# One ring place, three load orders and the folds of a two-layer block kernel

## The chip, the cores and the metric

The kernel runs on one core of a Trainium2 chip. A core has a matrix engine (TensorE, PE in the profile, with its weight loads as PEld) and four more engines with queues of their own: VectorE (DVE), ScalarE (ACT), GpSimd (POOL) and SyncE (SP, which here issues all transfers). The metric is the time of one execution on the device in microseconds.

## The reference

Two layers over 512 latent tokens and 256 context tokens, width 1024, feed-forward width 4096, float32. Cut to what matters here:

```python
for i in range(2):
    sh1, sc1, g1, sh2, sc2, g2 = split(silu(c) @ w_ada[i] + b_ada[i])   # and the same for ctx from c_ctx
    a = window_gqa(...) if i == 0 else diff_attention(...)
    x = layer_norm(alpha * x + g1 * a, ln1_g[i], ln1_b[i])
    fx = square(relu((x * (1 + sc2) + sh2) @ w1[i])) @ w2[i]
    x = layer_norm(alpha * x + g2 * fx, ln2_g[i], ln2_b[i])
    # layer 0 does the same to ctx; layer 1 needs only x
```

## The kernel before

**Numbers.** Each float32 product is made of three matmuls on values split in a rounded high part and the rest (mm3, L325 high x high, L326 and L327 the mixed ones). So every weight has to be prepared: a transfer brings it into a raw buffer, ACT rounds it (w_h, L264), DVE subtracts (w_l, L314); only then may PE use it. `wsplit` does that. Raw buffers come from a ring of three (tag raw, NRAW = 3); w_h and w_l from rings of four each (NH = 4).

**The order of work.** A planner in Python (class `Flow`) walks through jobs, with a cost for every operation and a latency after it (LNLAT = 6.0 us after a layer norm's normalise), and writes PE's order by hand from that. The order on ACT, DVE, POOL and SP is set by a scheduler by priority, which goes mostly by the place in the program. Each engine takes its queue strictly in order: what stands behind a waiting instruction waits too. All loads go through SP's one queue.

**The MLP (`mlp_pipe`).** It works on token blocks (tb) of 128: six in layer 0, four in layer 1. Blocks 0 to 5 of w1 are done plainly (`plain`). After that come the *pairs* q = 3 to 15 (`pair`): two blocks of w1 (a1, a2, the pair's raws) are quartered and combined to seven half weights (A11, A12, S2, S1, S3, S4, A22) so that seven products replace eight. POOL makes the sums (w_sum and sums in place, `part_sums`); `half` casts a half on ACT and subtracts on DVE into a tile w_half, and takes a place in the ring rhalf that PE gives back when the product (12 matmuls) is done. Between the products stand y groups: products of the second matrix w2 (y_ps), two weights for each of 7 chunks c and two halves of the 1024 columns. `sink` adds them to a tile fx; `fold` multiplies fx by the gate and adds it to the residual acc, both on POOL. `last_y` does the last chunk, whose sums `final` adds (`gated_add`: g_tmp on DVE at L583, then the add on DVE or POOL), and after half 1 of a block comes its layer norm (`moments`, `normalise` at L534, `ln_job`, which ends in transposes xn_t on PE, L549).

**Where things lie.** In layer 0 the pairs' two w1 raws are tiles of their own, and a half weight's tile is taken in turn from four pools (raw, bc, wh, wl): every fourth half lies in one of the three raw buffers. These also hold the y weights and the rows of w_adaT, the modulation of later stages, which the `filler` loads and DVE sums (custom instructions at L260), one step each time `R0.extra` draws. In layer 1 a fourth raw buffer, in the pool of its MLP, takes part in the rotation of all raws.

**The ends.** Layer 0's MLP ends with six loads of acc from m_spill (`tail`), two gate loads (g), the folds, the last y groups, and six layer norms, while `pre1` starts the qkv products of layer 1's attention. Layer 1's MLP begins with the last attention output weight (b_wo), the acc loads and the layer norm rows.

Of the kernel before, what the change touches and what calls it, by code (L numbers as in the profile page):

```python
# [19 lines left out]
P = 128  # L20
# [214 lines left out]
def hybrid_block(ctx: ExitStack, tc: tile.TileContext, t: dict, out: bass.AP):  # L235
# [296 lines left out]
    def normalise(a, st, dep):  # L532
        mv, rstd, d = moments(st, dep)
        nc.vector.tensor_scalar(out=a, in0=a, scalar1=mv[:, 0:1], scalar2=rstd, op0=ALU.subtract, op1=ALU.mult)  # L534
        return fl.op("D", dve(620), [d], LNLAT)


    def ln_job(pool, acc, tb, hx, A, B, ready, st, dep, keep=None):
        dep = normalise(acc, st, dep)
# [156 lines left out]
    def mlp_pipe(l, hx, ready, ntok, acc, get_gates, done, fx, T, R):  # L696
# [220 lines left out]
        def sink(c, half, tb, pt, p, slot):  # L917
            x = fx[tb][:, half * 512:half * 512 + 512]
            if (half, tb) not in fresh:
                fresh.add((half, tb))  # L920
                sm_.give(slot, ac(512, [p], nc.scalar.copy, out=x, in_=pt))
                if half == 0 and R.res:
                    R.res.pop(0)()
                return
            d = dv(512, [p], nc.vector.tensor_tensor, out=x, in0=pt, in1=x, op=ALU.add)
            sm_.give(slot, d)
            if c == 6 - half and gates:
                fold(half, tb, d)
# [13 lines left out]
        def last_y():  # L942
            def final(half, tb, pt, p, slot):
                r = gated_add(R.pool, lambda x: sm_.give(slot, x), acc[tb], half, pt, p, gates[0 if tb < NXB else 1],
                              half == 1 or l == 0)
# [17 lines left out]
            yield from before(1)  # L963
            if not gates:
                gates.extend((yield from get_gates()))
                for half in range(2):
                    for tb in range(ntb):
                        fold(half, tb, None)
# [61 lines left out]
        y_weights(0, 0)  # L1030
        y_weights(0, 1)
        weights(3, 4)
# [414 lines left out]
    with tc.tile_pool(name="mlp0", bufs=1, reuse_waits="tile") as pool:  # L1447
# [26 lines left out]
        class R0:  # L1474
            rhalf = Ring(fl, 4)
# [10 lines left out]
            def half_tile(self, n):  # L1486
                p_, tag, b = ((wpool, "raw", NRAW), (pool, "bc", 2), (wpool, "wh", NH), (wpool, "wl", NH))[n % 4]
                return p_.tile([P, 1024], F32R, name="w_half", tag=tag, bufs=b)
# [24 lines left out]
            def extra(self):  # L1513
                self.turn += 1
                if self.turn % 5 in (1, 3):
                    next(filler, None)
# [18 lines left out]
        def done2(tb, st, r):  # L1535
# [6 lines left out]
            fl.add(ln_job(pool, acc[tb], tb, st2["hx"], st2["A"], st2["B"], ready2, st, r), 0)  # L1542
# [379 lines left out]
    with tc.tile_pool(name="mlp1", bufs=1, reuse_waits="tile") as pool:  # L1922
        xraw["pool"] = pool
# [36 lines left out]
        class R1:  # L1960
# [4 lines left out]
            def pair_raws(self):  # L1965
                return raw_tile(), raw_tile()
# [107 lines left out]
```

## Time and profile before

| | |
|---|---|
| time, median of 3 runs | 1671.41 us (1671.11 to 1679.01) |
| the profiled execution's own time | 1669.35 us |
| its span, first to last instruction | 1667.6 us |
| granted TensorE clock, mean | 0.983 |
| PE busy | 1572.0 us, 94% |
| DVE, ACT, POOL busy | 1141.7, 790.1, 448.2 us |
| layer 0's MLP, pairs | about 455 to 815 us |
| layer 0's end, qkv of layer 1 | about 815 to 915 us |
| layer 1's MLP, pairs | about 1320 to 1620 us |

The profile is of one execution. In a row of a timeline stand the start, the duration, engine, line, operation, what it writes and reads, and in brackets how long the engine stood before it and what ended that. In a row of the waits stand the engine and line, what it waited for, the sum in us, how often, and the longest. A merged row (x2 and more) lasts from the first start to the last end.

### The profile page before, as it was taken

How to read it: one execution, taken by the hardware profiler on the slowest of the kernel's cores; microseconds unless marked ns; L12 is line 12 of the kernel's file. 1: busy time of each engine (PE TensorE's matmuls, PEld its weight loads, DVE VectorE, ACT ScalarE, POOL GpSimd, SP SyncE). 2: the span in 40 equal slices, each digit the busy share in tenths (PEclk: the TensorE clock that was granted, in tenths of full speed). 3: DMA queues.
4: the chain of work that ended last, by engine and by line, in shares of the span. 5: the costliest groups of instructions: out<-in, count | busy, mean ns of one | idle time of the engine just before them, and what ended most of it. 6: DMA issues, size and time to landing. Idle time of an engine off the chain costs nothing. (4 is left out here: it accounts for less than half of the span.)

```text
span 1667.6 us, 25133 instructions
## 1 busy us (share of the span) xinstructions
PE 1572.0 (94%) x9465; PEld 1385.1 (83%) x9465; DVE 1141.7 (68%) x2204; ACT 790.1 (47%) x1683; POOL 448.2 (27%) x364
## 2 busy tenths in 40 slices
PE   7899999999989997999998998999989899999997
PEld 5787777789878986988978898999877779999886
DVE  4555677699777687766486777776755875556577
ACT  3465676364433342334417555555542735555450
POOL 1334454106112111211550222221000033333463
PEclk9999999999999998999999999999999999999999
DMA  9110551533454334532522122211114332233221
GB/s 372 40 51 33 181 174 39 184 146 108 138 165 152 126 131 140 160 127 89 181 76 97 47 68 70 65 45 39 48 51 152 103 113 90 101 103 101 97 92 51
DMA packets 66434, 181.17 MB, mean 109 GB/s; under 512 B 7368, under 2 KB 13320, under 8 KB 66312
## 3 DMA queue, kind: packets, MB, share of 16 engines
q1 hardware_dynamic: 66312, 179.56, 31.6%
q8 instruction: 74, 1.21, 0.3%
q14 instruction: 48, 0.39, 0.1%
HBM read 168.49 MB, written 11.04 MB: 108 GB/s over the span
## 5 line engine op out<-in xcount | busy, mean ns | idle before, releaser
L325 PE MATMUL y_ps<-w_h,hid 128*128 128x512 f32 (+1 forms) x648 | 254.2, 392 | 15.2 <-ACT w_h L264 14.2
L326 PE MATMUL y_ps<-w_l,hid 128*128 128x512 f32 (+1 forms) x648 | 254.8, 393 | 6.7 <-DVE w_l L314 6.7
L327 PE MATMUL y_ps<-w_h,hid 128*128 128x512 f32 (+1 forms) x648 | 252.9, 390 | 0.0
L314 DVE TENSOR_TENSOR w_l<-w_raw,w_h 128x1024 fp32r<-128x1024 f32 (+1 forms) x133 | 164.0, 1242 | 81.8 <-ACT w_h L264 80.0
L264 ACT CAST w_h<-w_raw 128x1024 fp32r<-128x1024 f32 (+1 forms) x133 | 131.8, 1000 | 160.9 <-PE y_ps L327 64.0
L268 POOL TENSOR_TENSOR w_sum<-w_raw 128x512 f32<-128x512 f32 x26 | 57.6, 2217 | 478.6 <-DMA w_raw<-in_w 330.1
L325 PEld LDWEIGHTS y_ps<-w_h,hid 128*128 128x128 f32 x648 | 123.2, 190 | 39.5 <-ACT w_h L264 15.5
L326 PEld LDWEIGHTS y_ps<-w_l,hid 128*128 128x128 f32 x648 | 123.1, 190 | 31.4 <-DVE w_l L314 9.9
L264 ACT CAST w_half<-w_raw 128x512 fp32r<-128x512 f32 x130 | 78.5, 619 | 140.0 <-PE h_ps L327 69.8
L327 PEld LDWEIGHTS y_ps<-w_h,hid 128*128 128x128 f32 x648 | 123.1, 190 | 25.7
L325 PE MATMUL qkv_ps<-w_h,hx 128*128 128x384 f32 (+1 forms) x384 | 128.4, 334 | 0.6 <-ACT qT L264 0.5
L260 DVE TENSOR_TENSOR w_half<-w_raw,w_half 128x512 fp32r<-128x512 f32 x130 | 101.6, 795 | 39.0 <-ACT w_half L264 38.5
L327 PE MATMUL qkv_ps<-w_h,hx 128*128 128x384 f32 (+1 forms) x384 | 123.3, 321 | 0.0
L326 PE MATMUL qkv_ps<-w_l,hx 128*128 128x384 f32 (+1 forms) x384 | 123.2, 321 | 0.0
L268 POOL TENSOR_TENSOR e<-e,sm 128x512 f32<-128x512 f32 (+2 forms) x96 | 92.7, 979 | 108.4 <-DVE sm L260 89.8
L260 DVE TENSOR_TENSOR fx<-y_ps,fx 128x512 f32<-128x512 f32 x110 | 75.4, 686 | 49.8 <-PE y_ps L327 49.7
L260 DVE CUSTOM_DVE_ANT_0 w_raw<-w_raw,cB 128x512 f32<-128x512 f32 x112 | 81.5, 758 | 26.8 <-DMA w_raw<-in_w_adaT 26.7
L264 ACT ACTIVATE relu<-relu 128x384 f32<-128x384 f32 (+3 forms) x104 | 69.5, 671 | 50.6 <-DVE relu L260 49.3
L268 POOL TENSOR_TENSOR rope<-rope,rope 128x256 f32<-128x256 f32 (+1 forms) x40 | 35.3, 883 | 213.2 <-DVE rope L260 169.7
L264 ACT ACTIVATE e<-e,nm 128x513 f32<-128x513 f32 (+2 forms) x96 | 65.9, 687 | 32.9 <-DVE nm L260 26.2
L325 PE MATMUL h_ps<-hx1m,w_half 128*128 128x256 f32 x260 | 74.2, 286 | 7.1 <-DVE relu L260 4.0
L325 PEld LDWEIGHTS qkv_ps<-w_h,hx 128*128 128x128 f32 x384 | 73.3, 191 | 2.2 <-issue 1.2
(267 smaller groups left out, 4287.6 us busy)
## 6 DMA issues: line engine op xcount, KB each, us to landing
w_raw<-in_w SPq DMA_DIRECT2D x128, 512.0 KB, 3.6
w_raw<-in_w_adaT SPq DMA_DIRECT2D x56, 512.0 KB, 3.9
w_raw<-in_w_ada SPq DMA_DIRECT2D x24, 512.0 KB, 3.8
w_raw<-in_b_w SPq DMA_DIRECT2D x32, 384.0 KB, 3.3
raw<-in_w_ada SPq DMA_DIRECT2D x16, 512.0 KB, 9.6
w_raw<-in_a_wq SPq DMA_DIRECT2D x8, 512.0 KB, 7.0
w_raw<-in_a_wo SPq DMA_DIRECT2D x8, 512.0 KB, 4.3
w_raw<-in_b_wo SPq DMA_DIRECT2D x8, 512.0 KB, 4.7
```

The costliest lines, as they stand in the source:

```text
L260: fn(**kw)
L264: fn(**kw)
L268: fn(**kw)
L314: last["split"] = nc.vector.tensor_tensor(**kw)
L325: nc.tensor.matmul(out=o, lhsT=lh, rhs=rh, start=start, stop=False, **kw)
L326: nc.tensor.matmul(out=o, lhsT=lh, rhs=rl, start=False, stop=False, **kw)
L327: last["pe"] = nc.tensor.matmul(out=o, lhsT=ll, rhs=rh, start=False, stop=stop, **kw)
```

## The change

It does the following.

- Layer 0: the ring rhalf has three places (was four), and a half weight's tile is taken from bc, wh and wl in turn; no half lies in a raw buffer.
- `R0.extra` draws a step of the filler in three of eight turns (was two of five).
- Layer 1: the raws of all weights rotate over three buffers; the second raw of a pair has one buffer of its own in the pool of the MLP.
- In layer 1 the loads of pair 3's w1 are written ahead of the second y weights.
- `sink` folds only half 0, at chunk 6. Half 1 is folded in `last_y`, written behind the sums of the pairs.
- `final` in layer 0: half 0 and the last block add on DVE, half 1 of the other five blocks on POOL (all on DVE before). In layer 1 as before.
- The planner counts a latency of 2.5 us instead of 6.0 for the last block's layer norm at the end of layer 0.

The diff:

```diff
--- before.py
+++ after.py
@@ -529,14 +529,14 @@
         d = gp(0.47, [d], nc.gpsimd.tensor_tensor, out=rstd, in0=rstd, in1=mhalf[:, 0:1], op=ALU.pow)
         return mv, rstd, d
 
-    def normalise(a, st, dep):
+    def normalise(a, st, dep, lat=LNLAT):
         mv, rstd, d = moments(st, dep)
         nc.vector.tensor_scalar(out=a, in0=a, scalar1=mv[:, 0:1], scalar2=rstd, op0=ALU.subtract, op1=ALU.mult)
-        return fl.op("D", dve(620), [d], LNLAT)
-
-
-    def ln_job(pool, acc, tb, hx, A, B, ready, st, dep, keep=None):
-        dep = normalise(acc, st, dep)
+        return fl.op("D", dve(620), [d], lat)
+
+
+    def ln_job(pool, acc, tb, hx, A, B, ready, st, dep, keep=None, lat=LNLAT):
+        dep = normalise(acc, st, dep, lat)
         s = 0 if tb < NXB else 1
         tok = slice(tb * P, (tb + 1) * P)
         rs = []
@@ -924,7 +924,7 @@
                 return
             d = dv(512, [p], nc.vector.tensor_tensor, out=x, in0=pt, in1=x, op=ALU.add)
             sm_.give(slot, d)
-            if c == 6 - half and gates:
+            if c == 6 and gates:
                 fold(half, tb, d)
 
         def y_groups(groups):
@@ -942,7 +942,7 @@
         def last_y():
             def final(half, tb, pt, p, slot):
                 r = gated_add(R.pool, lambda x: sm_.give(slot, x), acc[tb], half, pt, p, gates[0 if tb < NXB else 1],
-                              half == 1 or l == 0)
+                              half == 1 if l else half == 0 or tb == ntb - 1)
                 st[tb], r = stats(acc[tb], half, r, st.get(tb))
                 if half:
                     done(tb, st[tb], r)
@@ -961,11 +961,12 @@
             y_weights(7, 0)
             yield from before(0)
             yield from before(1)
+            halves = (1,) if gates else (0, 1)
             if not gates:
                 gates.extend((yield from get_gates()))
-                for half in range(2):
-                    for tb in range(ntb):
-                        fold(half, tb, None)
+            for half in halves:
+                for tb in range(ntb):
+                    fold(half, tb, None)
             for tb in range(ntb):
                 yield sm_.ok
                 pt, slot = psm("y_ps"), sm_.take()
@@ -1028,8 +1029,10 @@
             for _ in sums:
                 pass
         y_weights(0, 0)
+        if l == 0:
+            y_weights(0, 1)
+        weights(3, 4)
         y_weights(0, 1)
-        weights(3, 4)
         yield from steps(2 * ntb)
         for q in range(3, 16):
             if q == R.gate_at:
@@ -1472,7 +1475,7 @@
             fl.add(ln_job(pool, acc[tb], tb, hx, A, B, ready, st, r, fx[tb]), 0)
 
         class R0:
-            rhalf = Ring(fl, 4)
+            rhalf = Ring(fl, 3)
             mixes = ((2, 2, 2, 0), (4, 4, 4, 0))
             gate_at, res = 16, None
             ahead, done, turn = 1, 0, 0
@@ -1484,7 +1487,7 @@
                 return self.ws
 
             def half_tile(self, n):
-                p_, tag, b = ((wpool, "raw", NRAW), (pool, "bc", 2), (wpool, "wh", NH), (wpool, "wl", NH))[n % 4]
+                p_, tag, b = ((pool, "bc", 2), (wpool, "wh", NH), (wpool, "wl", NH))[n % 3]
                 return p_.tile([P, 1024], F32R, name="w_half", tag=tag, bufs=b)
 
             def relu_tile(self):
@@ -1512,7 +1515,7 @@
 
             def extra(self):
                 self.turn += 1
-                if self.turn % 5 in (1, 3):
+                if self.turn * 3 % 8 < 3:
                     next(filler, None)
 
         def main0():
@@ -1539,7 +1542,8 @@
                 st2["hx"] = hx_big("hx1")
             if tb == NTB - 1:
                 st2["last"] = True
-            fl.add(ln_job(pool, acc[tb], tb, st2["hx"], st2["A"], st2["B"], ready2, st, r), 0)
+            fl.add(ln_job(pool, acc[tb], tb, st2["hx"], st2["A"], st2["B"], ready2, st, r, None,
+                          LNLAT if tb < NTB - 1 else 2.5), 0)
 
 
         def pre1():
@@ -1920,7 +1924,6 @@
         fl.run()
 
     with tc.tile_pool(name="mlp1", bufs=1, reuse_waits="tile") as pool:
-        xraw["pool"] = pool
         hl = [late.tile([P, 1024], F32R, name="w_" + x, tag="w" + x, bufs=1) for x in "hl"]
         acc = [pool.tile([P, D], F32, name="acc1", tag="acc", bufs=NXB) for _ in range(NXB)]
         for tb in range(NXB):
@@ -1963,7 +1966,7 @@
             gate_at, ahead = 10, 2
 
             def pair_raws(self):
-                return raw_tile(), raw_tile()
+                return raw_tile(), (pool.tile([P, 1024], F32, name="w_raw", tag="raw", bufs=1), rraw1.get(), rraw1)
 
             def sum_tile(self):
                 return late.tile([P, 1024], F32, name="w_sum", tag="wh", bufs=1)
```

What moves is told by the order of instructions. **SP, in the pairs of layer 0**, a stretch of nine loads with what each waits for. in_w1 are a pair's raws, in_w2 a y weight, in_w_adaT rows of the filler; DMAHW is an earlier transfer's end. Before:

```order
L275 DMA w_raw_4058<-in_w1 128x1024 [waits DVE_49]
L275 DMA w_raw_4059<-in_w1 128x1024 [waits DMAHW3_49]
L275 DMA w_raw_5409<-in_w_adaT 128x2x512 [waits DMAHW4_49,DMAHW1_49,DVE_49]
L275 DMA w_raw_5434<-in_w_adaT 128x2x512 [waits PE_49]
L275 DMA w_raw_5468<-in_w2 128x1024 [waits DMAHW5_49,DVE_49]
L275 DMA w_raw_5481<-in_w_adaT 128x2x512 [waits DMAHW7_49,DMAHW6_49,DVE_49]
L275 DMA w_raw_5506<-in_w_adaT 128x2x512 [waits PE_49]
L275 DMA w_raw_5544<-in_w2 128x1024 [waits DMAHW7_49,DVE_49]
L275 DMA w_raw_5605<-in_w_adaT 128x2x512 [waits DMAHW2_49,DMAHW0_49,DVE_49]
```

and now:

```order
L275 DMA w_raw_5460<-in_w2 128x1024 [waits DMAHW2_49,DMAHW1_49,DVE_49]
L275 DMA w_raw_5473<-in_w_adaT 128x2x512 [waits DMAHW3_49,DVE_49]
L275 DMA w_raw_5498<-in_w_adaT 128x2x512 [waits DMAHW4_49,DVE_49]
L275 DMA w_raw_5536<-in_w2 128x1024 [waits DMAHW5_49,DMAHW3_49,DVE_49]
L275 DMA w_raw_4058<-in_w1 128x1024 [waits DMAHW7_49,DVE_49]
L275 DMA w_raw_4059<-in_w1 128x1024 [waits DVE_49]
L275 DMA w_raw_5604<-in_w_adaT 128x2x512 [waits DMAHW4_49,DVE_49]
L275 DMA w_raw_5648<-in_w_adaT 128x2x512 [waits DMAHW0_49,DVE_49]
L275 DMA w_raw_5673<-in_w_adaT 128x2x512 [waits DMAHW2_49,DMAHW1_49,DVE_49]
```

Before, some loads wait for PE, to which a raw buffer with a half weight belongs; now loads wait for DVE and for earlier transfers.

**PE, at the end of layer 0**, around the transposes xn_t of the last blocks (acc_7904, 7905 and 7906 are blocks 3, 4 and 5). Now it reads:

```order
L325 MATMUL y_ps<-w_h,hid 128x512
L326 MATMUL y_ps<-w_l,hid 128x512
L327 MATMUL y_ps<-w_h,hid 128x512
L549 MATMUL xn_t<-identr,acc_7904 128x128 x4
L549 MATMUL xn_t<-identr,acc_7905 128x128 x8
L325 MATMUL qkv_ps<-w_h,hx_8181 128x384
L326 MATMUL qkv_ps<-w_l,hx_8181 128x384
L327 MATMUL qkv_ps<-w_h,hx_8181 128x384
L325 MATMUL qkv_ps<-w_h,hx_8181 128x384
L326 MATMUL qkv_ps<-w_l,hx_8181 128x384
L327 MATMUL qkv_ps<-w_h,hx_8181 128x384
L549 MATMUL xn_t<-identr,acc_7906 128x128 x8
L325 MATMUL qkv_ps<-w_h,hx_8181 128x384
```

The first rows are the last y matmuls. Before, 18 qkv matmuls stood between those and the transposes of acc_7905, and 54 more ahead of those of acc_7906:

```order
L325 MATMUL qkv_ps<-w_h,hx_8181 128x384
L326 MATMUL qkv_ps<-w_l,hx_8181 128x384
L327 MATMUL qkv_ps<-w_h,hx_8181 128x384
L549 MATMUL xn_t<-identr,acc_7906 128x128 x8
```

So the last block's transposes moved ahead of 66 of the 72 qkv matmuls.

**SP, in layer 1's MLP**, at pair 4 (w_raw_13620 and 13621 are its w1, 13639 and 13645 y weights, l2g and l2b the layer norm's rows). Before:

```order
L275 DMA w_raw_13620<-in_w1 128x1024
L275 DMA w_raw_13621<-in_w1 128x1024
L275 DMA l2g_16231<-in_lnrow 128x1024
L275 DMA l2b_16233<-in_lnrow 128x1024
L275 DMA w_raw_13639<-in_w2 128x1024
L275 DMA w_raw_13645<-in_w2 128x1024
L275 DMA w_raw_13823<-in_w1 128x1024
L275 DMA w_raw_13848<-in_w2 128x1024
```

and now:

```order
L275 DMA w_raw_13620<-in_w1 128x1024
L275 DMA w_raw_13639<-in_w2 128x1024
L275 DMA w_raw_13645<-in_w2 128x1024
L275 DMA l2g_16231<-in_lnrow 128x1024
L275 DMA l2b_16233<-in_lnrow 128x1024
L275 DMA w_raw_13823<-in_w1 128x1024
L275 DMA w_raw_13842<-in_w2 128x1024
L275 DMA w_raw_13621<-in_w1 128x1024
```

The two y weights moved ahead of l2g and l2b, the pair's second w1 behind them. At the start of that MLP, some 20 loads earlier, the first three loads of w1 stood ahead of the four of acc and of the last attention output weight (b_wo); now they stand behind these.

## The prediction

> **What bounds the kernel now.** I read first the page's busy times, then the waits of TensorE (PE), then the span in windows of 30 us, and then the timeline at the longest stalls.
>
> ```profile
> span 1667.6 us, 25133 instructions
> PE 1572.0 (94%) x9465; PEld 1385.1 (83%) x9465; DVE 1141.7 (68%) x2204; ACT 790.1 (47%) x1683; POOL 448.2 (27%) x364
> PE y_ps L325 <- ACT w_h L264: 16.1, 4, 9.5
> PE y_ps L326 <- DVE w_l L314: 7.5, 8, 2.5
> PE h_ps L325 <- DVE relu L260: 4.0, 1, 4.0
> ```
>
> PE is busy 94% and bounds the kernel, so a change can win only the 95.6 us in which it stands (1667.6 - 1572.0), and the time that it runs at a lower clock. The largest waits are those of the second MLP matrix (y_ps) for its cast (ACT, w_h) and its low part (DVE, w_l). The windows tell where. Columns: PE, PEld, DVE, ACT, POOL busy with counts, granted clock, DMA share, GB/s.
>
> ```profile
> 480.00:510.00 30.00, 25.52 (x120) 22.33 (x119) 20.83 (x39) 11.13 (x18) 6.52 (x4) 0.94 0.47 156
> 510.00:540.00 30.00, 28.15 (x139) 24.87 (x139) 19.76 (x37) 11.07 (x17) 4.28 (x3) 1.00 0.52 177
> 540.00:570.00 30.00, 30.00 (x153) 27.31 (x152) 22.79 (x42) 11.86 (x19) 7.20 (x5) 1.00 0.45 141
> 630.00:660.00 30.00, 22.76 (x113) 20.06 (x112) 23.37 (x58) 8.98 (x14) 4.38 (x4) 0.97 0.32 110
> 660.00:690.00 30.00, 27.33 (x120) 23.59 (x121) 20.67 (x42) 7.39 (x12) 5.83 (x4) 0.86 0.51 164
> 1380.00:1410.00 30.00, 30.00 (x194) 27.21 (x193) 16.73 (x25) 13.59 (x25) 8.51 (x6) 1.00 0.29 94
> ```
>
> A window of layer 0's pairs holds 153 matmuls when nothing stands; these four hold 120, 139, 113 and 120, 120 too few, which at 30/153 = 0.196 us each is 23.5 us. In layer 1's pairs PE has no gap (30.00): there the change can only lose.
>
> ```profile
> 657.58 0.34 SPq L275 DMA_DIRECT2D w_raw<-in_w  x1
> 661.11 1.04 ACT L264 CAST w_h<-w_raw 128x1024 fp32r<-128x1024 f32 x1 [6.79 <-DMA w_raw<-in_w]
> 662.21 0.80 PE L325 MATMUL y_ps<-w_h,hid 128*128 128x512 f32 x1 [9.45 <-ACT w_h L264]
> 663.47 0.80 PE L326 MATMUL y_ps<-w_l,hid 128*128 128x512 f32 x1 [0.46 <-DVE w_l L314]
> SPq L275 <- PE h_ps L327: 87.3, 19, 13.6
> ```
>
> That is the longest stall, back to front: PE waits for a cast, ACT stands in its queue for the load, and the load was issued 3.5 us before it landed, far too late. SP (SyncE) issues all loads in one queue, and a load goes out when one of three raw buffers is free. The last row is what holds that queue in 19 places, 87.3 us in sum: a raw buffer that PE has still to release, because a half weight lies in it.
>
> ```profile
> 664.00:667.00 3.00, 3.00 (x8) 2.31 (x7) 2.53 (x7) 0.00 (x0) 0.00 (x0) 0.50 0.70 233
> 843.00:846.00 3.00, 3.00 (x9) 2.37 (x8) 2.19 (x3) 0.00 (x0) 3.00 (x3) 0.54 0.27 96
> ```
>
> A stall costs more than its gap: after the 9.45 us the clock was 0.50, and after a gap of 2.51 us (quoted below) it was 0.54. Three microseconds at half clock lose 1.5.
>
> [...]
>
> **1. Layer 0's pairs.** Half weights no longer use a raw buffer; their ring has three places instead of four. In the new order no load of w_raw in this stretch waits for PE; they wait for DVE (the split or row sum that read the old contents). Of every five draws of the modulation rows (w_adaT), which share the raw buffers, the new rule also makes a little less: 3 in 8 for 2 in 5. The stalls of y_ps in this stretch are 16.1 + 7.5 less 2.51, 1.88 and 0.76, which lie elsewhere (below): 18.4 us; with the slow clock the windows gave 23.5.
>
> What could eat this is the ring of three:
>
> ```profile
> L264 ACT CAST w_half<-w_raw 128x512 fp32r<-128x512 f32 x130 | 78.5, 619 | 140.0 <-PE h_ps L327 69.8
> L260 DVE TENSOR_TENSOR w_half<-w_raw,w_half 128x512 fp32r<-128x512 f32 x130 | 101.6, 795 | 39.0 <-ACT w_half L264 38.5
> 539.93 0.35 PE L325 MATMUL h_ps<-hid,w_half 128*128 128x384 f32 x1
> 541.89 0.34 PE L327 MATMUL h_ps<-hid,w_half 128*128 128x384 f32 x1
> ACT w_half L264 <- PE h_ps L327: 93.8, 61, 5.5
> ```
>
> The third and fourth rows are the first and last of one product's 12 matmuls: 2.1 us. A half is cast (0.62) and split (0.80), 1.4 us together, after its place is free. With three places it may begin when the product three back is done, so the two products between leave at least 4.2 us, more where y work lies between. That leaves 2.8 us for the queues of ACT and DVE. Each place of the ring is now used by a third of the halves instead of a quarter, and two of the places are buffers of the y weights' own halves (wh, wl), so these too are released by PE. The 93.8 us in which ACT stands for PE before such a cast will grow, and behind it in ACT's queue stand the casts of y weights and the copies of relu. In the new order a y weight's cast stands behind work that PE releases some 40 matmuls ahead, where before it stood behind 7 to 24. I leave 3 to 6 us of stalls: six even pairs have their squared relu ready only just in time, at up to 0.5 us each, and the first pair starts with a half that waits for y. **Term: -18**, between 0 (all stalls stay in other places) and -23.5.
>
> **2. End of layer 0.** Two y weights now go ahead of the six loads of acc; the gates' loads go behind. The folds on POOL that need the gates start later, and the last adds of half 1 go to POOL for five of six blocks.
>
> ```profile
> 817.35 11.04 POOL L268 TENSOR_TENSOR fx<-fx,g 128x512 f32<-128x512 f32 x8 [11.93 <-DMA g<-gate_d]
> 839.33 2.28 DVE L314 TENSOR_TENSOR w_l<-w_raw,w_h 128x1024 fp32r<-128x1024 f32 x1
> 841.67 0.50 PE L326 MATMUL y_ps<-w_l,hid 128*128 128x512 f32 x1 [2.51 <-DVE w_l L314]
> 662.19 1.23 DVE L314 TENSOR_TENSOR w_l<-w_raw,w_h 128x1024 fp32r<-128x1024 f32 x1 [1.10 <-ACT w_h L264]
> ```
>
> The 2.51 us go, since the weight that was late is loaded ahead, and 1.5 of slow clock: -4 at best, 0 at worst; I take -2.5. POOL's eight multiplications take 1.38 us each, so 24 fold operations take 33 us and end near 864 instead of 854; the adds behind them (1.4 on POOL against 0.69) lengthen each layer norm by 0.7. PE covers that with the y groups of the next block; 0, at worst +2.
>
> [...]
>
> **3. The last block's layer norm.** The planner is told 2.5 us instead of 6 for it, so PE meets its transposes (xn_t) 6 qkv matmuls and 16 transposes after the last y matmul; before, 72 qkv matmuls lay between.
>
> ```profile
> 889.96 0.40 PE L327 MATMUL y_ps<-w_h,hid 128*128 128x512 f32 x1
> 894.94 0.68 DVE L583 TENSOR_TENSOR g_tmp<-y_ps,g 128x512 f32<-128x512 f32 x1
> 898.80 0.81 DVE L534 TENSOR_SCALAR acc<-acc,mv,rstd 128x1024 f32<-128x1024 f32 x1 [0.73 <-POOL rstd L268]
> 903.86 1.03 PE L549 MATMUL xn_t<-identr,acc 128*128 128x128 f32 x8
> 915.77 0.36 PE L1638 MATMUL kT_ps<-identr,sk 128*128 128x128 f32 x2 [3.15 <-DVE nlam L1601]
> ```
>
> The chain took 9.3 us from 890.3 to 899.6, of which 4.6 were spent behind other work of DVE and 4.7 (894.94 to 899.61) in itself. PE now has about 2.5 us to do meanwhile (6 x 0.17 and up to 1.4 for the transposes). So it stands at least 2.2 us, and 6.8 if DVE is as full as before; the first qkv products, whose inputs come just before, may add 1 to 2. Against that, the hx of the last block and with it the attention begin earlier, and the 3.15 us wait at 915.77 may shrink. **Term: +4**, between -1 and +9.
>
> **4. Layer 1.** Loads in another order and one own raw buffer for each pair's second w1.
>
> ```profile
> 1264.52 0.44 SPq L275 DMA_DIRECT2D w_raw<-in_b_wo  x1
> 1275.45 0.50 PE L325 MATMUL y_ps<-w_h,oT 128*128 128x512 f32 x1 [1.88 <-ACT w_h L264]
> 1360.83 0.93 SPq L275 DMA_DIRECT2D w_raw<-in_w  x2
> 1367.34 1.05 ACT L264 CAST w_h<-w_raw 128x1024 fp32r<-128x1024 f32 x1 [6.74 <-DMA w_raw<-in_w]
> 1371.98 0.58 PE L325 MATMUL h_ps<-hx1m,w_half 128*128 128x256 f32 x1 [4.04 <-DVE relu L260]
> 1610.59 0.58 PE L325 MATMUL h_ps<-hx1m,w_half 128*128 128x256 f32 x1 [3.01 <-ACT relu L264]
> ```
>
> The last weight of the attention's output (b_wo) was issued behind three loads of w1, 0.5 MB each; they now stand behind it: -2, between 0 and -2.6 (1.88 + 0.76 for its low part). At 1367 ACT stood 6.74 us for a y weight issued at 1360.83 behind two layer-norm rows that wait for residual sums; its load now goes ahead of them, so the 4.04 us stall goes, with 1 of slow clock: -4, between 0 and -5.5. In exchange one raw w1 is issued behind the rows; POOL sums it some 10 us later. At 1610 relu was late because folds on POOL ran among the last sums; the folds of half 1 now yield: -0.5, between +2 and -3. In the full windows the single own buffer is reloaded after its last half is cast, with nearly a pair's time ahead; 0, at worst the third rival.
>
> **Sum.** -18 - 2.5 + 4 - 2 - 4 - 0.5 = -23. The profiled execution took 1669.35 us (span 1667.6 and 1.75 around it), 2.06 below the median of 1671.41. So 1646 profiled and 1648.5 as a median; rounded up for what I cannot see, **1649**.
>
> **Rivals.**
> *The rows, not the halves, starve the loads (16%).* The load at 657.58 was late behind rows that DVE had not yet summed; with 3 draws in 8 the rows stay nearly as dense. Then the 9.45, 0.46 and 2.9 us of slow clock (30 us hold 120 instead of 153) stay, about 13, and the time is 1662. For it: DVE is busy 23.37 of 30 us in that window. Against it: 19 waits of the queue for PE.
> *The change doesn't do what it says (12%).* A ring of three makes ACT wait where SP did, the casts of y weights stand behind it, and term 1 falls to about -4; with term 3 at its bad end (+9) the sum is -4, or 1667.
> *Slower (9%).* The ring of three in the pairs: if the queues of ACT and DVE put 5.2 us instead of under 2.8 between a free place and a ready half, PE stands 2.4 us in one product of each of the 13 pairs, 31 us, against which the gains of 23 stand: 1680. It decides from 4.6 us on (13 x 1.8 = 23). For it: a split of w_l (1.23) and two row sums can stand ahead of a half on DVE. Against it: ACT is busy 9 to 12 of 30 us and DVE 20 to 23.
> *More than forecast (17%).* Terms 1 to 4 at their good ends, with a layer norm that costs nothing: -23.5 - 4 - 1 - 2.6 - 5.5 - 3 = -40, or 1631.
>
> **How the numbers follow.** The forecast holds 46%, its own range 1641 to 1657. Half a percent, 8.4 us, is about what a measurement can tell from no change: below 1663 is faster, above 1680 slower. Faster: 46 + 17 + 11 of the first rival's 16, 0.74. The second rival and the rest of the first lie within: 0.17. Slower: 0.09. The range runs from 1635 to 1668 and leaves out the slower case and the far end of the better one.
>
> **What would show it.** In the changed profile, windows between 480 and 690 with about 150 matmuls each; no row of SP that waits for PE h_ps in that stretch; y_ps L325 <- w_h below 5 us (term 1). No gap of y_ps near the end of layer 0 (term 2). A new wait of xn_t for the last block's normalise, or none at 3.15 us for nlam (term 3). No h_ps gap of 4 us some 95 us after layer 1's last b_wo (term 4). Wrong would be: new waits h_ps <- w_half in most pairs, or a window below 190 matmuls in layer 1's pairs.

## The result, and the profile after

The changed kernel takes 1660.59 us in the median of 7 runs (1656.2 to 1664.39), the kernel before 1671.11 in the 7 runs beside it: a ratio of 0.9929, with a 95% interval of 0.9907 to 0.9951. It is faster by 0.7%, or 10.5 us, where the forecast was 23 us and 1649; the first rival's 1662 is nearest.

The span is 9.1 us shorter. Its page, and the waits of PE between 340 and 850 us (engine, line, what was waited for, us in sum, times, longest):

```profile
span 1658.5 us, 25161 instructions
PE 1572.0 (95%) x9465; PEld 1384.3 (83%) x9465; DVE 1139.5 (69%) x2199; ACT 790.7 (48%) x1683; POOL 440.4 (27%) x369
PE h_ps L325 <- DVE relu L260: 3.4, 2, 1.8
PE y_ps L327 <- DVE hid L260: 2.6, 3, 1.2
PE y_ps L325 <- ACT hid L264: 2.4, 3, 1.2
PE y_ps L325 <- DVE fx L260: 0.9, 1, 0.9
SPq L275 <- PE h_ps L327: 8.8, 2, 8.4
```

PE's own work is unchanged. The waits of y_ps for w_h and w_l are gone from this stretch, and the load queue waits for PE's h_ps 8.8 us instead of 87.3, all of it behind 810, at the end of the pairs. In their place PE waits for relu and for hid. The windows of after, to be laid beside those of before:

```profile
450.00:480.00 30.00, 26.51 (x116) 22.71 (x117) 21.08 (x42) 11.19 (x18) 3.57 (x4) 0.89 0.54 172
480.00:510.00 30.00, 30.00 (x153) 27.32 (x152) 20.82 (x38) 12.70 (x20) 6.83 (x6) 1.00 0.44 144
510.00:540.00 30.00, 28.17 (x135) 25.51 (x134) 19.90 (x39) 10.77 (x18) 2.08 (x2) 0.94 0.43 141
660.00:690.00 30.00, 29.03 (x136) 25.69 (x137) 21.67 (x46) 8.33 (x14) 5.22 (x4) 0.94 0.50 159
870.00:900.00 30.00, 19.99 (x87) 15.51 (x87) 23.00 (x47) 21.20 (x59) 7.91 (x9) 0.80 0.21 79
1350.00:1380.00 30.00, 30.00 (x189) 27.06 (x188) 16.34 (x23) 15.60 (x28) 5.54 (x4) 1.00 0.46 161
```

The window at 480 is full now; those at 450, 510 and 660 are not. At 870, where layer 0 ends, PE is busy only 20 of 30 us, at a clock of 0.80: a hole that the kernel before did not have. At 1350 the stall of 4 us is gone.

Three stretches of PE's timeline, cut at the same instructions in every kernel, tell where the time went. They are in us: **A** from layer 0's first h_ps to its last (plain blocks and pairs), **B** from there to the first product with the output weights of layer 1's attention (oT; layer 0's end and that attention lie in it), **C** from there to layer 1's last h_ps.

| kernel | A | B | C |
|---|---|---|---|
| before | 485.2 | 387.8 | 402.4 |
| changed | 480.1 | 389.7 | 394.4 |
| difference | -5.1 | +1.9 | -8.0 |

From there to the last y both take 34.3 us. The rest of the difference, +2.0, lies ahead of A, where both run the same instructions. Over all profiles here A began between 346.8 and 350.7 us, so 2 us in one stretch of one profile is no finding. A varies too. Two kernels below in which PE and the load queue go through A in the same order (the one before with the ring of three, and the changed one with its rows in 2 of 5 turns) have 485.7 and 481.0, while the five with the changed kernel's code there lie between 478.1 and 480.1.

### The profile page after: what moved, and what is told of

Same layout as the page of the kernel before. It is cut to its first block, busy times and chain, and to the rows that moved or that the text cites. A ratio compares the mean times of both kernels' runs of the same rounds, so it can differ in the third digit from the quotient of the medians.

```text
span 1658.5 us, 25161 instructions
## 1 busy us (share of the span) xinstructions
PE 1572.0 (95%) x9465; PEld 1384.3 (83%) x9465; DVE 1139.5 (69%) x2199; ACT 790.7 (48%) x1683; POOL 440.4 (27%) x369
## 4 chain that ended last, share of the span: by engine, by line
PE 53%; DVE 17%; DMA 11%; issue 7%; ACT 6%; POOL 5%; SPq 0%; DVEq 0%; POOLq 0%; ACTq 0%
PE y_ps L325 6%; PE y_ps L327 6%; PE y_ps L326 6%; DMA w_raw<-in_w_adaT 6%; PE h_ps L325 4%; PE h_ps L326 4%; PE h_ps L327 4%; DVE w_raw L260 2%; DVE w_l L314 2%; PE o_ps L1359 2%; PE pT_ps L1377 2%; PE qkv_ps L325 2%; PE qkv_ps L326 2%; PE qkv_ps L327 2%; PE s_ps L1738 2%
## 5 line engine op out<-in xcount | busy, mean ns | idle before, releaser
L314 DVE TENSOR_TENSOR w_l<-w_raw,w_h 128x1024 fp32r<-128x1024 f32 (+1 forms) x133 | 158.1, 1199 | 61.7 <-ACT w_h L264 58.5
L260 DVE TENSOR_TENSOR w_half<-w_raw,w_half 128x512 fp32r<-128x512 f32 x130 | 105.9, 822 | 29.8 <-ACT w_half L264 28.1
L264 ACT COPY relu<-h_ps 128x384 f32<-128x384 f32 (+1 forms) x78 | 32.9, 422 | 119.5 <-PE h_ps L327 113.0
## 6 DMA issues: line engine op xcount, KB each, us to landing
w_raw<-in_b_w SPq DMA_DIRECT2D x32, 384.0 KB, 3.8
```

The source lines that it names most:

```text
L260: fn(**kw)
L264: fn(**kw)
L314: last["split"] = nc.vector.tensor_tensor(**kw)
```

## The experiments

Twelve kernels; each time is the median beside runs of the kernel before on the same chip, with the ratio to it. They ran on several chips, so two kernels are better compared by their ratios. A, B and C are of one profiled execution each; for the rows early in a pair that was the fastest of seven, 1653.04.

| kernel | us | ratio, 95% interval | A | B | C |
|---|---|---|---|---|---|
| latency back to 6.0 | 1661.37 | 0.9933 (0.9910 to 0.9955) | 478.1 | 391.6 | 397.7 |
| adds on DVE | 1653.95 | 0.9900 (0.9870 to 0.9929) | 478.1 | 385.1 | 394.2 |
| both | 1657.29 | 0.9911 (0.9887 to 0.9935) | 479.6 | 382.8 | 396.2 |
| before + ring of three | 1668.79 | 0.9977 (0.9960 to 0.9995) | 485.7 | 388.5 | 398.3 |
| changed, rows 2 of 5 | 1662.96 | 0.9939 (0.9914 to 0.9964) | 481.0 | 389.6 | 393.5 |
| changed, ring of four | 1677.32 | 1.0018 (0.9998 to 1.0039) | 498.4 | 383.3 | 395.1 |
| adds on DVE, quarter of the rows | 1642.63 | 0.9807 (0.9773 to 0.9842) | 462.0 | 386.9 | 397.4 |
| adds on DVE, row steps in two draws | 1658.24 | 0.9896 (0.9865 to 0.9928) | 479.4 | 385.8 | 398.0 |
| adds on DVE, layer 1 as before | 1660.41 | 0.9927 (0.9909 to 0.9945) | 479.1 | 385.4 | 400.0 |
| adds on DVE, sums without loads | 1654.95 | 0.9895 (0.9872 to 0.9919) | 477.3 | 387.9 | 397.5 |
| adds on DVE, rows early in a pair | 1662.71 | 0.9940 (0.9918 to 0.9962) | 482.3 | 381.7 | 393.7 |
| quarter of the rows, ring of four | 1637.62 | 0.9795 (0.9751 to 0.9839) | 462.4 | 384.0 | 396.3 |

### The end of layer 0: latency or adds

The hole at 870, in PE's timeline of the changed kernel, and behind it what DVE and POOL did:

```profile
873.38 0.63 PE L549 MATMUL xn_t<-identr,acc 128*128 128x128 f32 x4 [2.49 <-POOL rstd L268]
883.57 0.66 PE L549 MATMUL xn_t<-identr,acc 128*128 128x128 f32 x4 [2.77 <-DVE g_tmp L583]
892.38 0.63 PE L549 MATMUL xn_t<-identr,acc 128*128 128x128 f32 x4 [0.64 <-DVE g_tmp L583]
895.93 0.69 PE L325 MATMUL qkv_ps<-w_h,hx 128*128 128x384 f32 x1 [2.93 <-ACT w_h L264]
897.80 0.69 PE L326 MATMUL qkv_ps<-w_l,hx 128*128 128x384 f32 x1 [1.18 <-DVE w_l L314]
865.61 1.28 POOL L268 TENSOR_TENSOR acc<-acc,g_tmp 128x512 f32<-128x512 f32 x1
866.92 0.69 DVE L260 BATCH_NORM_STATS2 bn<-acc 128x6 f32<-128x512 f32 x1 [8.60 <-POOL acc L268]
```

Five gaps, 10.0 us, and the slow clock (0.80 in that window). The last two rows show the first cause: the add of half 1 stood on POOL behind the folds, and DVE stood 8.6 us for it with the layer norm.

Two parts of the change meet here. The first kernel undoes the latency:

```diff
-                          LNLAT if tb < NTB - 1 else 2.5), 0)
+                          LNLAT), 0)
```

> The changed kernel with the planner's latency for the last block's layer norm at the end of layer 0 back at 6.0 us (2.5 in the change). In the order of PE only the last block's transposes move, 12 qkv matmuls later; those of block 4 stay right behind the last y matmul. Theory A (the latency is what makes PE stand at the end of layer 0): the 10 us of gaps between 870 and 900 go for the most part, 5 to 8 us faster than the change, 1653 to 1656. Theory B (the adds of half 1 on POOL move the transposes, the latency little): 0 to 3 us faster, 1658 to 1661.

The second undoes the adds on POOL:

```diff
-                              half == 1 if l else half == 0 or tb == ntb - 1)
+                              half == 1 or l == 0)
```

> The changed kernel with the last adds of layer 0 on DVE for both halves again, as before the change; the latency stays at 2.5. In the order of PE the transposes of block 4 stand again 18 qkv matmuls behind the last y matmul and those of block 5 37 rows later. Theory A (latency): PE still stands for the last block, 0 to 3 us faster than the change. Theory B (adds on POOL): the waits of xn_t for POOL's rstd and for g_tmp go (2.5, 2.8, 0.6) and most of the slow clock in that stretch, 5 to 9 us faster, 1651 to 1656.

The third undoes both.

> Both undone, adds on DVE and latency 6.0, everything else of the change kept: the end of layer 0 in the order of before. Theories A and B agree: 5 to 10 us faster than the change, 1650 to 1656; what it gains over the better of the two single ones is the rest of the other's share.

The latency alone changes nothing that can be measured (1661.37; B 391.6). With the adds on DVE B falls from 389.7 to 385.1, and to 382.8 with the latency back as well. That fits theory B. A planner that counts the adds on POOL moves the last block's transposes far ahead: they stand behind 6 of the 72 qkv matmuls in the changed kernel and behind 18 with the latency undone, but behind 54 with the adds undone and 72 with both. And the adds themselves stand behind the folds.

B as a whole varies between kernels with the adds on DVE and the ring of three (381.7 to 388.5), so its first part is the better measure. From A's end to the 400th matmul the three kernels with the adds on POOL and the ring of three take 92.2 to 92.8 us, the eight with the adds on DVE and that ring 83.7 to 86.7, and the kernel before 85.0. One more kernel, which comes below for another reason, parts the folds from the rest. The changed kernel with the ring of four has the same adds on POOL and the same place of the transposes, but its folds begin 14.6 us ahead of A's end, where in the changed kernel they begin 0.7 us behind it. They are done when the first add comes:

```profile
878.55 1.29 POOL L268 TENSOR_TENSOR acc<-acc,g_tmp 128x512 f32<-128x512 f32 x1 [10.42 <-DVE g_tmp L583]
```

POOL stood 10.42 us before it, and the waits of 2.49 and 2.77 us are gone. It takes 88.5 us to the 400th matmul, and its B is 383.3. So about 4 of the some 7 us there are the queue behind the folds, as far as one profile of it can tell; the rest, from the order of PE or the adds, was not parted.

With the adds on DVE the same stretch of the timeline reads:

```profile
877.11 0.50 PE L325 MATMUL y_ps<-w_h,hid 128*128 128x512 f32 x1 [2.62 <-DVE g_tmp L583]
892.31 0.81 DVE L534 TENSOR_SCALAR acc<-acc,mv,rstd 128x1024 f32<-128x1024 f32 x1 [0.73 <-POOL rstd L268]
894.25 1.03 PE L549 MATMUL xn_t<-identr,acc 128*128 128x128 f32 x8
905.40 0.36 PE L1642 MATMUL kT_ps<-identr,sk 128*128 128x128 f32 x2 [2.12 <-DVE sk L260]
```

The last block is normalised at 893.1 and its transposes at 894.25 wait for nothing, although the latency is still 2.5. By the median this is the fastest kernel of all that leave nothing out, 1653.95. It is ahead of the kernel before; its interval and that of the changed kernel still overlap a little (0.9870 to 0.9929, 0.9907 to 0.9951). Between it and the one with both undone (1657.29) the intervals decide nothing.

### Layer 0's pairs: ring, rows or DVE

First the ring of three alone, on the kernel before:

```diff
-            rhalf = Ring(fl, 4)
+            rhalf = Ring(fl, 3)
...
-                p_, tag, b = ((wpool, "raw", NRAW), (pool, "bc", 2), (wpool, "wh", NH), (wpool, "wl", NH))[n % 4]
+                p_, tag, b = ((pool, "bc", 2), (wpool, "wh", NH), (wpool, "wl", NH))[n % 3]
```

> The kernel before with one part of the change alone: layer 0's half weights in a ring of three that leaves the raw buffers alone. Theory C (the ring gives what layer 0's pairs gained): the stalls of y_ps on w_h and w_l between 480 and 690 go, others of relu and hid behind DVE's row sums come, net 5 to 10 us faster than before, 1661 to 1666. Rival D (the thinner drawing of the rows gives it): no difference from before, 1669 to 1673. The forecast's own term would be 18 us, 1653.

1668.79 is 0.2% faster than before, and A is as long as before (485.7). Its waits of PE between 360 and 850:

```profile
PE y_ps L327 <- DVE hid L260: 4.3, 4, 2.5
PE y_ps L325 <- ACT hid L264: 2.9, 5, 1.1
PE h_ps L325 <- DVE relu L260: 2.7, 2, 2.3
PE h_ps L327 <- DVE w_l L314: 1.9, 1, 1.9
PE h_ps L327 <- DVE w_half L260: 1.7, 1, 1.7
```

The y weights are no longer late, and A is no shorter: most of the waits are now for hid and relu. Neither theory C's 5 to 10 us nor the forecast's 18 came; rival D's "no difference" is nearest. Then the changed kernel with one of the two parts undone: the rows in 2 of 5 turns,

```diff
-                if self.turn * 3 % 8 < 3:
+                if self.turn % 5 in (1, 3):
```

> The changed kernel with the rows drawn in 2 of 5 turns again, as before the change. Time of layer 0's MLP from its first product to its last (first to last h_ps): 485.2 us before, 480.1 with the change, 485.7 with the ring of three alone. Theory C (ring and thinner rows only gain together): about 485 here, so 4 to 6 us slower than the change, 1664 to 1667. Rival D2 (the difference between 480 and 485.7 is of the runs, or of layer 1's side): about 480, same time as the change, 1659 to 1662.

and the ring of four:

```diff
-            rhalf = Ring(fl, 3)
+            rhalf = Ring(fl, 4)
...
-                p_, tag, b = ((pool, "bc", 2), (wpool, "wh", NH), (wpool, "wl", NH))[n % 3]
+                p_, tag, b = ((wpool, "raw", NRAW), (pool, "bc", 2), (wpool, "wh", NH), (wpool, "wl", NH))[n % 4]
```

> The changed kernel with the ring of four, every fourth half weight in a raw buffer again; rows drawn in 3 of 8 turns as in the change. Theory C (both are needed): the stalls of y_ps on w_h and w_l come back, first to last h_ps about 485, 1664 to 1668. Rival D (the thinner rows alone make the gain): about 479, same as the change, 1658 to 1662. The forecast's term (the raw buffers that PE holds cost 18 us): about 495 and 1675.

The thinner rows are worth nothing that can be told (A 481.0 against 480.1, 1662.96 against 1660.59). With the ring of four and the thinner rows A is 18.3 us longer and the kernel no faster than before. Its waits in that stretch:

```profile
PE y_ps L325 <- ACT w_h L264: 14.5, 4, 5.5
PE y_ps L326 <- DVE w_l L314: 5.5, 7, 2.1
PE gate_t L456 <- DVE mods L260: 5.0, 2, 4.1
```

So theory C (both parts are needed) fell, and so did rival D (the rows alone); what came is near what the forecast's own term had said here, 495 and 1675. The cut is not clean: A is 18.3 us longer, but behind A the same 215 y matmuls take 56.8 us instead of 62.1, as the folds begin earlier (above). A and B together are 11.9 us longer than in the changed kernel, and the time 16.7 (15 by the ratios). So beside these rows the ring is worth 12 to 17 us, though 5.0 us of A is a wait for the modulation, which the kernel before with its denser rows did not have. Beside the old rows it was worth at most 4 in A (485.2 against 485.7 and 481.0, two kernels with the same code in this stretch). What the ring brings hangs on how the rows fall.

What is left in A? In the changed kernel relu's add waits on DVE, here at 449.83, behind sums over rows of w_adaT (custom instructions on w_raw and cB):

```profile
445.83 0.69 DVE L260 CUSTOM_DVE_ANT_0 ada_pr<-w_raw,cB 128x512 f32<-128x512 f32 x1 [4.42 <-DMA w_raw<-in_w_adaT]
446.56 1.65 DVE L260 CUSTOM_DVE_ANT_0 ada_pr<-w_raw,cB 128x512 f32<-128x512 f32 x1
448.15 1.75 DVE L260 CUSTOM_DVE_ANT_0 w_raw<-w_raw,cB 128x512 f32<-128x512 f32 x1
449.83 0.55 DVE L260 TENSOR_TENSOR relu<-h_ps,relu 128x384 f32<-128x384 f32 x1
450.43 0.45 PE L325 MATMUL h_ps<-hx0m,w_half 128*128 128x384 f32 x1 [1.57 <-DVE relu L260]
```

DVE stood 4.42 us for a row's transfer, then summed, and only then came to relu, for which PE stood 1.57 us. That looked like the transfer's fault (theory E). Two of the sums took 1.65 and 1.75 us instead of 0.69, beside sums on POOL, which is part of the delay here; at the waits for hid near 460 and 660 POOL was idle and the sums took 0.69. Two kernels test the rows as a whole and the way they are drawn. One loads and sums only every fourth step of the rows, so the later modulation is not the reference's:

```diff
                 for k in range(0, KT, 2):
-                    raw, rg, rr = raw_tile()
-                    d = dma(1024, [rg], out=raw.rearrange("p (k c) -> p k c", k=2),
...
-                    for s in range(n):
...
+                    if k == 0:
+                        raw, rg, rr = raw_tile()
+                        d = dma(1024, [rg], out=raw.rearrange("p (k c) -> p k c", k=2),
...
+                        for s in range(n):
...
```

> The changed kernel with the adds on DVE, but of the rows of w_adaT only every fourth step is loaded and summed; the rest is left out (mods stay zero there), so the modulation of the later stages is not the reference's. Theory E (what is left of stalls in layer 0's pairs comes from row sums that wait on DVE for their transfer, ahead of relu's adds and hid's splits): the gaps between 440 and 720 (about 12 us and slow clock behind them) go, first to last h_ps 462 to 468 against 478, time 1639 to 1645. Rival F (the ring of three itself makes those gaps: halves wait for PE and relu behind them): they stay, 475 to 478, 1651 to 1654.

The other draws load and sums in two turns:

```diff
                             in_=t["w_adaT"][l, m, k:k + 2, :, c_].rearrange("k p c -> p k c"))
+                    yield
...
-                if self.turn * 3 % 8 < 3:
+                if self.turn * 6 % 8 < 6:
```

> The changed kernel with the adds on DVE, and each step of the rows split in two draws: the load in one turn, its sums on DVE written in the next; drawn in 6 of 8 turns, so as many rows in the same time. Theory E: the sums stand later in DVE's queue and their transfer has landed when they come to the head, so DVE idles less for rows and the gaps behind relu and hid shrink: first to last h_ps 468 to 474, 1644 to 1650. Rival F, or the longer hold of the raw buffers by rows: same or slower than with the adds on DVE alone, 1653 to 1660.

With a quarter of the rows A is 462.0 and PE stands nowhere in the pairs. In the stretch from 425 to 785 us, columns as in the windows, this kernel and behind it the changed one:

```profile
425.00:785.00 360.00, 360.00 (x1806) 326.50 (x1805) 192.05 (x308) 143.05 (x228) 68.65 (x49) 1.00 0.27 85
```

```profile
425.00:785.00 360.00, 350.75 (x1716) 314.13 (x1715) 259.72 (x508) 134.91 (x216) 66.08 (x45) 0.98 0.43 141
```

PE is busy all 360 us at a clock of 1.00, DVE 192 instead of 260. But drawing load and sums apart brings nothing that can be told (A 479.4; 1658.24). Nor does it do what it was meant for: between 425 and 785 DVE still stands 61.8 us for rows, against 63.9 with the adds on DVE alone. So is it the row's transfer or the time that DVE sums? The next kernel keeps the number of sums and takes away three of four loads; those sums read a constant tile, and the modulation is again not the reference's:

```diff
-                    raw, rg, rr = raw_tile()
+                    if k == 0:
+                        raw, rg, rr = raw_tile()
...
+                    else:
+                        d = None
...
-                            src = raw[:, i * 512:i * 512 + 512]
+                            src = raw[:, i * 512:i * 512 + 512] if k == 0 else cB[1 - s]
```

> The changed kernel with the adds on DVE, but of four steps of the rows only the first is loaded; the other three do the same number of sums on DVE from a constant tile, so the later modulation is not the reference's. It keeps DVE's work and takes away the transfers and their hold of raw buffers. Measured with the rows of every fourth step alone, loads and sums: no gap in layer 0's pairs, first to last h_ps 462. Theory E1 (DVE idles at the head of its queue for a row's transfer, relu and hid wait behind): 462 to 466, 1639 to 1646. Rival E2 (it is DVE's time that the sums take): the gaps behind relu and hid stay, 472 to 478, 1650 to 1655.

A is 477.3, as with all loads, and the waits are the old ones. Its waits of PE between 360 and 850, and its largest group of sums on DVE between 425 and 785, with the largest of the kernel with all loads (adds on DVE) behind it (count, busy us, mean ns, us idle ahead of them):

```profile
PE y_ps L327 <- DVE hid L260: 2.8, 3, 1.2
PE h_ps L325 <- DVE relu L260: 2.6, 1, 2.6
PE y_ps L325 <- ACT hid L264: 1.4, 2, 0.7
L260 DVE CUSTOM_DVE_ANT_0 ada_pr<-cB,cB 128x512 f32<-128x512 f32 x106 | 85.2, 804 | 1.9
L260 DVE CUSTOM_DVE_ANT_0 w_raw<-w_raw,cB 128x512 f32<-128x512 f32 x100 | 74.2, 769 | 43.4 <-DMA w_raw<-in_w_adaT 43.3
```

The sums no longer wait (1.9 us idle ahead of 106 of them; all waits for rows are 4.1 us instead of 63.9), yet PE waits for hid and relu as before. Theory E1 fell; E2 holds: it is DVE's time in the sums, 138 of them at 0.7 to 0.8 us each in this stretch, that stands ahead of relu's adds and hid's splits.

Drawing the rows at another place of the pair,

```diff
-                R.extra()
+                if i < 2:
+                    R.extra()
...
                 if q == 15:
                     R.tail()
-                R.extra()
...
-            yield from pair(q, lambda i: steps(m[i]), ahead)
+            yield from pair(q, lambda i: steps(m[i], i), ahead)
...
-                if self.turn * 3 % 8 < 3:
+                if self.turn * 5 % 8 < 5:
```

> The changed kernel with the adds on DVE, and the rows drawn only in the first two of a pair's stretches of y work (5 of 8 turns there), none in the third, which stands ahead of the last relu and the splits to hid, so about as many rows in all. Theory E1: the splits to hid no longer stand behind rows that are on their way, the gaps of y_ps for hid near 460 and 660 go, first to last h_ps 466 to 474, 1642 to 1650. Rival J (rows drawn closer together hold all raw buffers and delay the y weights behind them in the queue): y_ps waits for w_h again, 480 to 490, 1656 to 1666.

brought no gain: the median is 1662.71, longer than with the adds on DVE alone though the intervals overlap a little, and A is 482.3. The waits for relu and hid are 12.4 us in sum (5.3, 4.1 and 3.0) instead of 7.3, and there is none for w_h. Theory E1 missed; rival J's numbers came (480 to 490, 1656 to 1666) without its mechanism. More of the wait is now at relu's adds (5.3 us instead of 2.8), which the rows meet there.

Last, the quarter of the rows with the ring of four, which puts half weights back into the raw buffers:

```diff
-            rhalf = Ring(fl, 3)
+            rhalf = Ring(fl, 4)
...
-                p_, tag, b = ((pool, "bc", 2), (wpool, "wh", NH), (wpool, "wl", NH))[n % 3]
+                p_, tag, b = ((wpool, "raw", NRAW), (pool, "bc", 2), (wpool, "wh", NH), (wpool, "wl", NH))[n % 4]
```

> The kernel with the adds on DVE and a quarter of the rows (the rest of the loads and sums left out, so the later modulation is not the reference's), and the ring of four again: every fourth half weight in a raw buffer. The same with the ring of three: no gap in layer 0's pairs, first to last h_ps 462.0, 1642.6. Theory K (half weights that PE holds starve the loads by themselves): y_ps still waits for w_h and w_l, 468 to 480, 1649 to 1660. Rival L (three raw buffers are enough for halves and y weights, it takes the rows to starve them): no gap or under 2 us, 462 to 464, 1641 to 1645.

A is 462.4, so the ring makes no difference without the rows. Its row for the load queue and the row of its window:

```profile
SPq L275 <- PE h_ps L327: 106.6, 19, 14.9
425.00:785.00 360.00, 359.76 (x1805) 325.96 (x1805) 202.44 (x318) 142.85 (x229) 71.04 (x48) 1.00 0.26 87
```

The queue waits for PE's half weights longer than in the kernel before (106.6 against 87.3 us, 19 times in both), and PE loses nothing there. Rival L holds in A. The 5 us between the medians of the two kernels with few rows lie outside A, and their ratios can't be told apart (0.9807 and 0.9795).

### Layer 1

The kernel with the adds on DVE, and the raw rotation, the order of loads and the folds of layer 1 as before the change:

```diff
-            if c == 6 and gates:
+            if c == 6 - half and gates:
...
-        if l == 0:
-            y_weights(0, 1)
-        weights(3, 4)
         y_weights(0, 1)
+        weights(3, 4)
...
+        xraw["pool"] = pool
...
-                return raw_tile(), (pool.tile([P, 1024], F32, name="w_raw", tag="raw", bufs=1), rraw1.get(), rraw1)
+                return raw_tile(), raw_tile()
```

> The changed kernel with the adds of layer 0 on DVE, and all of layer 1's part undone: the fourth raw buffer in the common rotation, the order of pair 3's w1 and the y weights, and the folds of half 1 as before. Measured for it: from the first product of the last attention weight (oT) to the last h_ps of layer 1, 402.4 us before and 394.4 with the change. Theory G (layer 1's part is worth what the forecast said, 6.5 us): 400 to 403 in that stretch, the wait for b_wo (1.9 us) and the 4 us wait of h_ps for relu come back, and the time is 4 to 8 us above the kernel with the adds on DVE, 1658 to 1662. Rival H (later gaps at the end of layer 1's pairs and the later plain weights take it back): 394 to 397, 1653 to 1656.

C is 400.0 against 394.2, and the time 1660.41 against 1653.95 (by the ratios some 4.5 us, with intervals that overlap): theory G. The waits that the forecast named came back, if smaller than before the change, in PE's timeline:

```profile
1266.41 0.49 PE L325 MATMUL y_ps<-w_h,oT 128*128 128x512 f32 x1 [0.85 <-ACT w_h L264]
1267.67 0.50 PE L326 MATMUL y_ps<-w_l,oT 128*128 128x512 f32 x1 [0.76 <-DVE w_l L314]
1359.87 0.39 PE L325 MATMUL h_ps<-hx1m,w_half 128*128 128x256 f32 x1 [2.53 <-DVE relu L260]
```

C varies between profiles with the same code in it (393.5 to 398.0 in the eleven with the change's layer 1, mean 395.8; 398.3, 402.4 and 400.0 in the three without, mean 400.2), so that one pair of profiles says little of the size; the means are 4.4 us apart. The waits are sharper: that of h_ps for relu, 2.53 to 4.04 us at the start of the pairs, stands in each of the three and in none of the eleven.

## Why the prediction was right and wrong

**What bounds the kernel** was read rightly: A with a quarter of the rows is 462.0, 23.2 us under the kernel before, and the windows had given 23.5. The time fell inside the forecast's outer range, 1635 to 1668, but under half of the 23 us came; what is missing, some 13 us, lies in term 1.

**Term 1 (-18)** was the step that failed; 5 us came. The stalls of y_ps on w_h and w_l did go. What failed is the sentence that 3 to 6 us of stalls would be left by the ring: some 18 us were left (480.1 against 462.0). PE stands 12.8 us in A against 3.5 with few rows, and most of the rest of the 18 goes with the slower clock behind those waits: from 425 to 785 the changed kernel has a clock of 0.98 and 1716 matmuls, the one with few rows 1.00 and 1806. These 90 are some 18 us (at 360/1806 each), of which PE stands 9.25. The forecast had relu ready at most 0.5 us late in six pairs, and row sums on DVE only ahead of a half weight, in the slower rival. In fact DVE's row sums stand ahead of relu and hid; in the kernel before, PE stood for late y weights instead, which may have given relu and hid the time (argued, not shown). The row of evidence, 87.3 us in which the load queue waits for PE, was no price: with few rows 106.6 us of the same wait cost nothing. In these runs the half weights cost time only together with the rows (A 498.4 against 480.1 with the rows in 3 of 8 turns, 462.4 against 462.0 with a quarter of them).

**The first rival (the rows, 1662)** gave the time almost exactly, but by luck, not by its mechanism. The 9.45 us stall that it kept is gone, and it is not the loads that the rows hold up now but DVE.

**Term 2 (-2.5)** and **term 3 (+4)** together were +1.5; B grew by 1.9. The sum was right by luck, the cause wrong. The order of PE was laid to the latency of 2.5 us, but mostly the adds on POOL had made it: of the 66 qkv matmuls that the last transposes passed, undoing the latency gives back 12 and undoing the adds 48. "PE covers that with the y groups of the next block; 0, at worst +2" failed: the adds stood behind the folds, and cost 4.6 us (B 389.7 against 385.1). The forecast had the folds end 10 us later, near 864 (865.7 came), but counted 0.7 for each add behind them, not the wait for their end. The 2.51 us gap went as forecast (0.48); it came back with the ring of four, 2.51 us. A slower DVE beside POOL is another candidate: in the prediction's rows of before, the split w_l took 2.28 us at 839.33, beside the folds on POOL, and 1.23 at 662.19, where POOL stood idle. Some 1 us more of a DVE operation beside each of the five adds on POOL would be 5 us (an estimate from these two rows), near that size. But the changed kernel's trace shows more of the queue on POOL: 8.6 us of waiting for an add of 1.28, and with the folds done earlier (ring of four) the same adds on POOL go with a B of 383.3.

**Term 4 (-6.5 in all)** was right in kind, and near in size: C shrank by 8.0 in the one comparison, by 5.8 in the other, and by 4.4 between the means. The gaps at b_wo and the one at 1372 went. At the end of layer 1's pairs, ACT and PE in the changed kernel:

```profile
1585.66 1.04 ACT L264 CAST w_h<-w_raw 128x1024 fp32r<-128x1024 f32 x1 [4.26 <-DMA w_raw<-in_w]
1587.55 0.52 PE L325 MATMUL h_ps<-hx_sum,w_half 128*128 128x256 f32 x1 [2.15 <-ACT relu L264]
1602.73 0.39 PE L325 MATMUL h_ps<-hx1m,w_half 128*128 128x256 f32 x1 [2.16 <-ACT relu L264]
```

A y weight is late there now and relu stands behind its cast, 2.15 us. This gap, 0.65 to 2.15 us, stands in all eleven profiles with the change's layer 1 and in none of the other three; the forecast had counted nothing for it. Which of layer 1's parts made it was not tried. The last wait is 2.16 where it was 3.01, but over the profiles it is 1.80 to 4.98 us with the change and 2.78 to 4.04 without, so the half microsecond that the forecast gave the folds is not shown.

**The slower rival** did not come: in no profile does PE wait in most pairs for a half weight.

## What to carry to other kernels

Here a stall that was removed showed the next one in line (w_h and w_l, then relu and hid); before a whole gap is counted, ask which engine was catching up during it. The cheapest test is to take the suspected work away and look whether the stage reaches its floor: with a quarter of the rows A fell to 462 with either ring, which no change of the ring had told. A long wait of a transfer queue need not be a price by itself (106.6 us of it cost nothing here), and an order that a planner wrote is to be laid to the edit that made it, by undoing one edit at a time.

## What the runs showed of the hardware

In the changed kernel the clock fell behind waits of under 2 us, behind several close together and behind one alone, but not behind each. Five waits of 0.39 to 1.57 us end between 450 and 466. After the first, 1.57, the clock stayed at 1.00; after the other four, within 5 us, it fell to 0.50. Behind a single wait of 1.83 us, which ends at 521.76, it fell to 0.50 too. PE's rows, and two windows with the clock in the third column from the end:

```profile
463.66 0.51 PE L325 MATMUL y_ps<-w_h,hid 128*128 128x512 f32 x1 [0.81 <-ACT hid L264]
465.56 0.79 PE L327 MATMUL y_ps<-w_h,hid 128*128 128x512 f32 x1 [1.16 <-DVE hid L260]
521.76 0.45 PE L325 MATMUL h_ps<-hx0m,w_half 128*128 128x384 f32 x1 [1.83 <-DVE relu L260]
467.00:470.00 3.00, 3.00 (x9) 2.32 (x8) 2.62 (x5) 0.00 (x0) 1.28 (x1) 0.50 0.78 253
524.00:526.00 2.00, 2.00 (x8) 2.00 (x8) 2.00 (x3) 0.77 (x2) 0.00 (x0) 0.50 0.15 39
```

The matmul behind the last of the four took 0.79 us, the one at 463.66 took 0.51, and those behind it followed each other every 0.43 us, where they had done so every 0.23. In the window from 450 to 480, with a clock of 0.89, PE stands 3.5 us; it holds 116 matmuls instead of 153, which is 7.3 us, so the slow clock cost about as much as the waits. The prediction was right to count a slow clock on top of its stall of 2.51 us (0.54 behind it).

In the changed kernel's stretch from 425 to 785 none of the 114 row sums on DVE that ran beside no operation of POOL took over 0.69 us. Of all 135, 14 took 1.12 to 1.78 us, and all 14 ran beside an operation of POOL.
